# Hybrid decoder layer on one core: group A's second FFN takes its input without the norm's root, which multiplies gates and ups instead, and silu becomes one operation in the FFNs with quads

## The chip, the core and the metric

One core of a Trainium2 chip runs the whole layer in one launch, in fp32. The metric is the time of one execution on the device, in microseconds (us). TensorE (PE in the profile) multiplies matrices, VectorE (DVE), ScalarE (ACT) and GpSimd (POOL) work on elements, SyncE (SP) issues the transfers (DMA).

## The reference, cut to what matters

```python
D_MODEL = 1024; SEQ = 1024; N_META = 16; D_FF = 2816

def rms_norm(x, g):
    y = x * lax.rsqrt(jnp.mean(x * x, axis=-1, keepdims=True) + RMS_EPS)
    return y * g

def swiglu(h, w_gate, w_up, w_down):
    return (jax.nn.silu(h @ w_gate) * (h @ w_up)) @ w_down

h = concatenate([meta, x])                      # 1040 tokens
n = rms_norm(h, ffn1_norm)
h = h + 0.5 * swiglu(n, ffn1_w_gate, ffn1_w_up, ffn1_w_down)
proj = rms_norm(h, mix_norm) @ w_in
sb_out = stick_breaking_attention(q, k, v)      # 8 heads of 64, from proj
rw_out = rwkv7_time_mix(the other columns of proj)   # 8 heads of 64, a recurrence over the tokens
h = h + concatenate([sb_out, rw_out]) @ w_out
n = rms_norm(h, ffn2_norm)
h = h + 0.5 * swiglu(n, ffn2_w_gate, ffn2_w_up, ffn2_w_down)
return rms_norm(h, final_norm)[N_META:]
```

The root of rms_norm is one number per token, `lax.rsqrt(...)`; a product `n @ w` is that number times `(h * g) @ w`.

## The kernel before

**Products.** Each fp32 factor is split into two halves in TensorE's fast fp32 type: a high one (names that end in h or hi: nh, ah, whi) and the rest (nl, al, wlo). A product is three matrix instructions, high by high, low by high and high by low. Activations lie with the features on the 128 partitions and the tokens along the row; D_MODEL is 8 tiles (k), D_FF 22 tiles (f). Weights arrive as 512 KB tiles wraw of 128x1024; ScalarE copies the high half (whi), VectorE subtracts for the low one (wlo).

**Stages.** The tokens are two groups: A (16 meta and 512) and B (512). In order: FFN1 of A, projections of A, FFN1 of B with the mixer (attention and recurrence) of A laid between its products, projections of B, w_out of A (from about 1266 us to 1317 us), FFN2 of A with the mixer of B between its products and w_out of B late in it (1808 to 1853 us), FFN2 of B (from 1899 us), and the last norm. FFN1 of A and FFN2 of B are the two "fast" ones: most of their f tiles go in pairs, as quads (`gates2`, `ups2`), in which sums of weight and activation blocks stand for some of the products (qh, ql, t1, t2); sg is their sigmoid, cc the ring of tiles that it comes from.

**One FFN.** `gate` makes pg = n·w_gate in PSUM for a chunk of tokens (two chunks of 256 for the first f's, then 512 columns at once), takes sigmoid(pg) into sl on ScalarE, and multiplies sl by pg on VectorE. `up` makes pu, multiplies sl by it and splits the result into ah and al. `downs` makes pd from four f's at a time and adds half of it to h. 24 gates of this kind are in FFN2 of A: 4 on 256 columns, 20 on 512.

**The norm.** `norm_add` squares each new h tile (nsq) and adds up (nacc); `norm_sums` sums over partitions with TensorE (nps) and takes the inverse root on VectorE in a chain of small steps (fst); `norm_root` spreads it over the partitions (nyp on TensorE, ny by ScalarE). `norm_end` then makes, for each of the 8 k's, nf = h·gain·ny on VectorE, nh on ScalarE, and nl on VectorE or POOL in turn. In FFN2 of A this is done apart for two chunks of 256 tokens, as `norm_task("n2_0", i, ...)`, started by `hookC` when the chunk's last h tile has been added. `norm_raw`, which the norm ahead of the projections already uses, makes nh = h·gain and nl = h·gain − nh with no root.

**Order.** One instruction stream for each engine is written beforehand by a planner (`Clock`): tasks yield what they need, and the planner keeps a model of the engines' clocks and chooses what is issued next. All instructions are recorded through one helper, so nearly every row of the profile says L101 and is told apart by its tiles. Every engine works in the order given. Tiles with a tag share a ring of `bufs` buffers: nsq has 4, sl 2, ny 1, cc a few. Names in the mixer that the prediction uses: t, pz, pp, tt, lw, pe (decays and a small inverse), px, rsv, us (the recurrence over blocks), sgl and pgate (its output gate, read back from DRAM at lod), lt (read back from Ld).

Of the kernel before, what the change touches and what calls it, by code (L numbers as in the profile page):

```python
# [16 lines left out]
P = 128  # L17
# [434 lines left out]
class Ker:  # L452
# [279 lines left out]
    def norm_add(self, s, h, k, cols, now=True):  # L732

        nc, tp = self.nc, self.fp
        w = cols.stop - cols.start
        with self.urgent() if now else nullcontext():
            if s["k"] == 0:
                t = s["tile"]() if s["tile"] else tp.tile([P, 272], F32, tag="nacc", bufs=2, name="nacc")
                s["acc"] = t[:, :w]
                nc.scalar.activation(s["acc"], h[:, k, cols], AF.Square)  # L740
            else:
                sq = tp.tile([P, 272], F32, tag="nsq", bufs=4, name="nsq")[:, :w]
                nc.scalar.activation(sq, h[:, k, cols], AF.Square)
                if s["k"] >= KT - s["late"] and now and not s["tile"]:
                    s["last"].append(sq)
                    self.hold((sq,))
                else:
                    nc.vector.tensor_tensor(out=s["acc"], in0=s["acc"], in1=sq, op=ALU.add)
        s["k"] += 1
# [42 lines left out]
    def norm_end(self, s, h, cols, gain, n, bank, now=True):  # L792

        nc, tp = self.nc, self.fp
        w = cols.stop - cols.start
        ys = []

        def new():
            ys.append(tp.tile([P, 272], F32, tag="ny", bufs=1, name="ny"))
            self.hold(ys)  # L800
            return ys[0][:, :w]
        yield from self.norm_root(s, w, new, bank, ("ny", 1))
        y = ys[0][:, :w]
        for k in range(KT):
            yield from self.room(tp, ("sl", 2) if k % 2 else ("nsq", 4))
            with self.urgent() if now else nullcontext():
                f = tp.tile([P, 512], F32, tag="sl", bufs=2, name="nf")[:, :w] if k % 2 else tp.tile([P, 272], F32, tag="nsq", bufs=4, name="nf")[:, :w]
                nc.vector.scalar_tensor_tensor(f, h[:, k, cols], self.v(gain, k), y, ALU.mult, ALU.mult)
                self.split(n[0][k][:, cols], n[1][k][:, cols], f, nc.gpsimd if k % 2 else None)
        self.drop(ys)  # L810
        yield self.need(*[x for k in range(KT) for x in (n[0][k][:, cols], n[1][k][:, cols])])
# [41 lines left out]
            self.drop((xn,))  # L853


    def ffn(self, nm, h, n, chunks, edge, bank, first=None, hook=None, wx=False, poll=None, resid=None, done=None, wy=False, fast=False, once=False):

# [29 lines left out]
        def gate(w, c0, c1):  # L889
            pg = yield from mm(*w, "pg", c0, c1)  # L890
            with self.urgent():
                sl = tp.tile([P, 512], F32, tag="sl", bufs=2, name="sl")[:, :c1 - c0]
                nc.scalar.activation(sl, pg, AF.Sigmoid)
                nc.vector.tensor_tensor(out=sl, in0=pg, in1=sl, op=ALU.mult)
            self.hold((sl,))
            return sl

# [9 lines left out]
        def gates(f):  # L907
            if poll:
                yield from poll(f)
            w = yield from gu(gw, f)  # L910
            sls = []
            for c in chunks:
                sl = yield from gate(w, *c)
                sls.append(sl)
            return sls
        two = lambda w, f: (w[:, :, f * P:f * P + P], w[:, :, f * P + P:f * P + 2 * P])

        def gates2(f):

            yield lambda: self.fast and self.fast.k == 4  # L920
            c = self.fast
            x2 = yield from self.quad("pg", two(gw, f), bank)
            for x in x2:
                yield from self.room(c.p, ("cc", c.nc))
                with self.urgent():
                    sg = c.p.tile([P, 2 * c.w], F32, tag="cc", bufs=c.nc, name="sg")
                    nc.scalar.activation(sg, x, AF.Sigmoid)
                    nc.vector.tensor_tensor(out=x, in0=x, in1=sg, op=ALU.mult)
            self.hold(x2)
            return x2  # L930

# [52 lines left out]
        for part in PARTS:  # L984
# [49 lines left out]
            if f1 == NFT and hook:  # L1034
                yield from last(part)
            elif not (fast and f1 >= QF):
                for q in range(f1 - f0):
                    yield from downs(part, q)
        for op, x, f in quad_order() if fast else ():
            if op == "d":  # L1040
# [184 lines left out]
    def plan(self):  # L1225
# [13 lines left out]
        def ffn(nm, poll=False, wx=False, fast=False, once=False):  # L1239
# [7 lines left out]
            for f0, f1 in PARTS:  # L1247
# [16 lines left out]
                if f1 < NFT:  # L1264
# [1 line left out]
                        F["woutat"] = f1  # L1266
                        yield from wout(True)
                    yield gu("gate", f1)
                yield from [down(f0, f1, q) for q in range(f1 - f0)]
            for op, x, f in quad_order() if fast else ():  # L1270
                if op == "d":
                    yield down(*x, f)
# [785 lines left out]
    def body(self):  # L2058
# [64 lines left out]
        def xfirst():  # L2123

            with self.urgent():
                nc.sync.dma_start(out=g1r, in_=A["ffn1_norm"])
                xs.extend(xload(0, *b) for b in blks[:2])
                nc.scalar.activation(g1w, self.ones[:, 0:1], AF.Square)
            self.g1p = []
            for q in range(2):  # L2130
                yield self.need(g1r, bank=self.tbank)
                ps = tb("pg1")
                self.g1p.append(ps)
                self.hold((ps,))
                nc.tensor.matmul(ps, lhsT=self.ones[0:1, :], rhs=g1r[:, 512 * q:512 * q + 512], start=True, stop=True)
            F["g1b"] = True
            yield lambda: F.get("xn")
            for q, ps in enumerate(self.g1p):
                nc.scalar.activation(self.g1b[:, 512 * q:512 * q + 512], ps, AF.Copy)
            self.drop(self.g1p)  # L2140
# [130 lines left out]
        def wait(key):  # L2271
            def w(i):
                yield lambda: F.get((key, i))
            return w
# [62 lines left out]
        def poll(f=None):  # L2337

            if F.get("woutat", -1) == f and not F.get("wout"):
# [3 lines left out]

                def hook(i, m):
                    if hk(i, m):
                        norm_task("n2_1", i, f2["h"], chB, "g2", f2["n"], not late)
                yield from self.wout(f2["h"], f2["n"], hook, lambda i: F.get(("mixb", i)), late)

        def dense():
# [37 lines left out]
            F["stage"] = True  # L2387
            addC = add("n2_0", h, chB)

            def hookC(i, m):  # L2390
                if addC(i, m):
                    norm_task("n2_0", i, h, chB, "g2", n)
            yield from self.wout(h, n, hookC, lambda i: F.get(("mixl", i)))
            fsum = []

# [6 lines left out]
            def done(m):  # L2402
# [3 lines left out]
                if F["fsum"]:  # L2406
                    for i in range(2):
                        addF(i, m)
            yield from self.ffn("ffn2", h, n, ch, chB, bank, wait("n2_0"), None, None, poll, done=done)
            yield lambda: "woutat" in F  # L2410
            yield from poll()

            def fin0():
                yield lambda: F.get(("n2_1", 1))
                for i in range(2):
                    for m in () if F["fsum"] else range(KT):
                        yield from self.room(fp, ("nsq", 4))
                        addF(i, m)
                    yield from self.final(ssq["fin0", i], 0, h, slice(*chB[i]), bank, (fp, ("sl", 2)))
                    self.drop(fsum[i:i + 1])  # L2420
# [52 lines left out]
```

## Time and profile before

| | us |
|---|---|
| runs | 2272.85 (median), 2270.57, 2273.04 |
| profiled execution, its time | 2273.33 |
| its span in the trace | 2271.4 |
| TensorE busy | 2239.5 (99%) |
| VectorE busy | 1566.0 (69%) |
| ScalarE busy | 1085.4 (48%) |
| GpSimd busy | 555.8 (24%) |
| mean granted clock of TensorE | 0.994 |

A row of a timeline reads: start in us, duration in us, engine, line, operation, out<-in, shapes, and in brackets how long the engine was idle before it and what released it. A row of waits reads: engine and tile that waited, who released it, us in total, times, longest. A row of a group gives the count, the least, median and largest duration in ns, and the first and last start in us. In a stretch, the granted clock of TensorE is a share of full speed; a TensorE row counts its instruction's time from start to modelled end, and consecutive matrix instructions overlap, so what one costs is the distance between two starts.

### The profile page before, as it was taken

How to read it: one execution, taken by the hardware profiler on the slowest of the kernel's cores; microseconds unless marked ns; L12 is line 12 of the kernel's file. 1: busy time of each engine (PE TensorE's matmuls, PEld its weight loads, DVE VectorE, ACT ScalarE, POOL GpSimd, SP SyncE). 2: the span in 40 equal slices, each digit the busy share in tenths (PEclk: the TensorE clock that was granted, in tenths of full speed). 3: DMA queues.
4: the chain of work that ended last, by engine and by line, in shares of the span. 5: the costliest groups of instructions: out<-in, count | busy, mean ns of one | idle time of the engine just before them, and what ended most of it. 6: DMA issues, size and time to landing. Idle time of an engine off the chain costs nothing.

```text
span 2271.4 us, 41476 instructions
## 1 busy us (share of the span) xinstructions
PE 2239.5 (99%) x16303; PEld 1979.7 (87%) x16303; DVE 1566.0 (69%) x2673; ACT 1085.4 (48%) x2157; POOL 555.8 (24%) x700
## 2 busy tenths in 40 slices
PE   8999999999999999999999999999999999999998
PEld 7999999999878888778788987887877899899998
DVE  6888887475666655676476877547777656688885
ACT  6444444434343534555434554445666335354444
POOL 1322120013133231431012415324443001231110
PEclk9999999999999999999999989999999999999999
DMA  5543332545633233322545524333221433333332
GB/s 166 180 112 103 93 94 78 170 132 145 182 105 106 74 100 98 100 88 67 172 141 175 159 79 128 86 92 116 76 85 52 144 112 126 91 109 109 105 90 78
DMA packets 407384, 256.54 MB, mean 113 GB/s; under 512 B 44941, under 2 KB 392293, under 8 KB 407190
## 3 DMA queue, kind: packets, MB, share of 16 engines
q1 hardware_dynamic: 407190, 253.90, 38.2%
q8 instruction: 128, 2.10, 0.4%
q14 instruction: 66, 0.54, 0.1%
HBM read 219.85 MB, written 33.99 MB: 112 GB/s over the span
## 4 chain that ended last, share of the span: by engine, by line
PE 94%; DVE 2%; ACT 1%; DMA 1%; issue 1%; SPq 0%; POOL 0%; DVEq 0%; ACTq 0%; POOLq 0%
PE pd L101 34%; PE pu L101 22%; PE pg L101 21%; PE pwo L101 4%; PE px L101 3%; PE po L101 2%; PE pz L101 2%; PE pat L101 2%; PE pG L101 1%; DVE wlo L101 1%; PE psw L101 0%; DMA wraw<-in_ffn_w_gate_dram 0%; SPq L101 0%; PE pp L101 0%; ACT whi L101 0%
## 5 line engine op out<-in xcount | busy, mean ns | idle before, releaser
L101 ACT ACTIVATE whi<-wraw 128x1024 fp32r<-128x1024 f32 x314 | 330.6, 1053 | 333.9 <-PE pd L101 208.8
L101 DVE TENSOR_TENSOR wlo<-wraw,whi 128x1024 fp32r<-128x1024 f32 (+1 forms) x312 | 401.0, 1287 | 88.6 <-ACT whi L101 83.8
L101 PE MATMUL pd<-ah,whi 128*128 128x512 f32 (+2 forms) x944 | 325.9, 345 | 2.6 <-DVE h L101 1.2
L101 PE MATMUL pd<-ah,wlo 128*128 128x512 f32 (+2 forms) x944 | 319.3, 338 | 1.2 <-DVE wlo L101 1.2
L101 PE MATMUL pd<-al,whi 128*128 128x512 f32 (+2 forms) x944 | 318.5, 337 | 0.1
L101 PE MATMUL pd<-nh,whi 128*128 128x256 f32 (+7 forms) x648 | 210.6, 325 | 0.3 <-DVE st L101 0.2
L101 PE MATMUL pu<-nh,whi 128*128 128x512 f32 (+3 forms) x576 | 207.0, 359 | 0.0
L101 PE MATMUL pd<-nl,whi 128*128 128x256 f32 (+7 forms) x648 | 204.5, 316 | 0.0
L101 PE MATMUL pd<-nh,wlo 128*128 128x256 f32 (+7 forms) x648 | 204.4, 315 | 0.0
L101 PE MATMUL pg<-nh,whi 128*128 128x512 f32 (+3 forms) x536 | 199.8, 373 | 0.5 <-ACT nh L101 0.5
L101 PEld LDWEIGHTS pd<-ah,whi 128*128 128x128 f32 x944 | 177.6, 188 | 25.5 <-issue 3.1
L101 PE MATMUL pu<-nh,wlo 128*128 128x512 f32 (+3 forms) x576 | 198.6, 345 | 0.6 <-DVE wlo L101 0.6
L101 PE MATMUL pu<-nl,whi 128*128 128x512 f32 (+3 forms) x576 | 198.7, 345 | 0.0
L101 PEld LDWEIGHTS pd<-ah,wlo 128*128 128x128 f32 x944 | 177.6, 188 | 22.5 <-DVE wlo L101 2.1
L101 PEld LDWEIGHTS pd<-al,whi 128*128 128x128 f32 x944 | 177.8, 188 | 17.9 <-DVE al L101 0.7
L101 PE MATMUL pg<-nl,whi 128*128 128x512 f32 (+3 forms) x536 | 190.5, 355 | 0.9 <-DVE nl L101 0.9
L101 PE MATMUL pg<-nh,wlo 128*128 128x512 f32 (+3 forms) x536 | 190.2, 355 | 0.0
L101 POOL TENSOR_TENSOR qs<-wraw 128x512 f32<-128x512 f32 x60 | 101.5, 1697 | 359.3 <-DVE ql L101 142.3
L101 DVE SCALAR_TENSOR_TENSOR h<-pd,h 128x256 f32<-128x256 f32 (+1 forms) x200 | 107.4, 541 | 75.3 <-PE pd L101 73.9
L101 POOL TENSOR_TENSOR al<-sl,ah 128x512 fp32r<-128x512 f32 (+2 forms) x47 | 75.6, 1609 | 323.3 <-ACT ah L101 323.2
L101 PEld LDWEIGHTS pd<-nh,whi 128*128 128x128 f32 (+2 forms) x648 | 120.1, 185 | 13.0 <-issue 3.1
L101 PEld LDWEIGHTS pd<-nh,wlo 128*128 128x128 f32 (+2 forms) x648 | 120.1, 185 | 8.7
(393 smaller groups left out, 5624.6 us busy)
## 6 DMA issues: line engine op xcount, KB each, us to landing
wraw<-in_ffn_w_gate_dram SPq DMA_DIRECT2D x90, 512.0 KB
wraw<-in_ffn_w_up_dram SPq DMA_DIRECT2D x90, 512.0 KB
wraw<-in_ffn_w_down_dram SPq DMA_DIRECT2D x88, 512.0 KB
wraw<-in_w_in_dram SPq DMA_DIRECT2D x54, 512.0 KB
wraw<-in_w_out_dram SPq DMA_DIRECT2D x18, 512.0 KB
s<-rkvd SPq DMA_DIRECT2D x18, 256.0 KB
raw<-qkvd SPq DMA_DIRECT2D x16, 264.0 KB
raw<-qkvd SPq DMA_DIRECT2D x16, 256.0 KB
```

The lines of the kernel that those rows point to most:

```text
L101: self._c.trace(self._n, op, lambda: f(*a, **k), out, [x for x in args if isinstance(x, bass.AP)], k)
```

## The change

- `ffn` gets `root=`. Group A's second FFN is called with it; its input n is now h·gain in two halves, made by `norm_raw` from `hookC` for all 8 k's at once when the last w_out tile of a chunk has been added.
- A new task `norm2(i)` computes the root of a chunk into its half of `root2`, a tile of the ring ny, which is held until the last gate (f = 21) has been written.
- In `gate`, pg is multiplied by the root in PSUM before the sigmoid, and sl by the root once more after silu, which scales the up.
- In FFNs with quads, sigmoid and multiply become one Silu on ScalarE, in `gate` and, in place in PSUM, in `gates2`; sg is gone.
- nsq has 3 buffers instead of 4; the norm of group B's second FFN takes its pieces as urgent for chunk 0 only; group B's w_out may also be started between the downs of the last part.

```diff
     def norm_end(...):
-            ys.append(tp.tile([P, 272], F32, tag="ny", bufs=1, name="ny"))
+            ys.append(tp.tile([P, 512], F32, tag="ny", bufs=1, name="ny"))
...
-    def ffn(..., fast=False, once=False):
+    def ffn(..., fast=False, once=False, root=None):
...
         def gate(w, c0, c1):
             pg = yield from mm(*w, "pg", c0, c1)
             with self.urgent():
+                if root:
+                    nc.vector.tensor_tensor(out=pg, in0=pg, in1=root()[:, c0:c1], op=ALU.mult)
                 sl = tp.tile([P, 512], F32, tag="sl", bufs=2, name="sl")[:, :c1 - c0]
-                nc.scalar.activation(sl, pg, AF.Sigmoid)
-                nc.vector.tensor_tensor(out=sl, in0=pg, in1=sl, op=ALU.mult)
+                nc.scalar.activation(sl, pg, AF.Silu if fast else AF.Sigmoid)
+                if not fast:
+                    nc.vector.tensor_tensor(out=sl, in0=pg, in1=sl, op=ALU.mult)
+                if root:
+                    nc.vector.tensor_tensor(out=sl, in0=sl, in1=root()[:, c0:c1], op=ALU.mult)
             self.hold((sl,))
             return sl
...
+            if root and f == NFT - 1:
+                self.drop((root(),))
...
         def gates2(f):
             for x in x2:
-                yield from self.room(c.p, ("cc", c.nc))
                 with self.urgent():
-                    sg = c.p.tile([P, 2 * c.w], F32, tag="cc", bufs=c.nc, name="sg")
-                    nc.scalar.activation(sg, x, AF.Sigmoid)
-                    nc.vector.tensor_tensor(out=x, in0=x, in1=sg, op=ALU.mult)
+                    nc.scalar.activation(x, x, AF.Silu)
...
                 def hook(i, m):
                     if hk(i, m):
-                        norm_task("n2_1", i, f2["h"], chB, "g2", f2["n"], not late)
+                        norm_task("n2_1", i, f2["h"], chB, "g2", f2["n"], i == 0)
...
+            root2 = []
+
             def hookC(i, m):
                 if addC(i, m):
-                    norm_task("n2_0", i, h, chB, "g2", n)
+                    for k in range(KT):
+                        self.norm_raw(h, k, slice(*chB[i]), "g2", n)
+                    task(norm2(i), ("n2_0", i))
+
+            def norm2(i):
+                if i == 0:
+                    yield from self.room(fp, ("ny", 1))
+                    root2.append(fp.tile([P, 512], F32, tag="ny", bufs=1, name="root2"))
+                    self.hold(root2)
+                yield lambda: root2
+                yield from self.norm_root(ssq["n2_0", i], 256, lambda: root2[0][:, 256 * i:256 * i + 256], bank)
...
-            yield from self.ffn("ffn2", h, n, ch, chB, bank, wait("n2_0"), None, None, poll, done=done)
+            yield from self.ffn("ffn2", h, n, ch, chB, bank, wait("n2_0"), None, None, poll, done=done, root=lambda: root2[0])
```

**How the order moves.** TensorE's sequence from about 400 us to the end of group A's w_out, and its last rows, stay as they are. Three places show what moved; in the rows the numbers behind a name tell tiles apart (nh_147 and nh_148 hold the first and the second four k's), and "x2" is the count of like instructions.

TensorE at the end of group A's w_out, where the gate of f = 0 begins, before:

```order
L101 MATMUL pwo<-nh_148,wlo 128x256
L101 MATMUL nps<-ones,nacc 128x1 x2
L101 MATMUL pz<-t_15294,ab 32x32 x16
L101 MATMUL nps<-ones,nsq 128x1 x2
L101 MATMUL pg<-nh_147,whi 128x256
L101 MATMUL pg<-nl_149,whi 128x256
```

And now:

```order
L101 MATMUL pwo<-nh_148,wlo 128x256
L101 MATMUL nps<-ones,nacc 128x1 x2
L101 MATMUL pz<-t_15250,ab 32x32 x16
L101 MATMUL pg<-nh_147,whi 128x256
L101 MATMUL pg<-nl_149,whi 128x256
L101 MATMUL pg<-nh_147,wlo 128x256
```

The first gate's products no longer come behind the second chunk's last sum (nps from nsq), which now stands nine products later.

VectorE at the same place, before:

```order
L101 SCALAR_TENSOR_TENSOR nf<-h,vec,ny 128x256
L101 TENSOR_TENSOR h<-pwo,h 128x256
L101 TENSOR_TENSOR nl_150<-nf,nh_148 128x256
L101 TENSOR_TENSOR nacc<-nacc,nsq 128x256
L101 SCALAR_TENSOR_TENSOR nf<-h,vec,ny 128x256 x3
L101 SCALAR_TENSOR_TENSOR t_15294<-pp,half,t_15294 32x8x16 x2
L101 TENSOR_TENSOR nl_150<-nf,nh_148 128x256
L101 TENSOR_TENSOR h<-pwo,h 128x256
L101 TENSOR_TENSOR wlo<-wraw,whi 128x1024 x2
```

And now:

```order
L101 TENSOR_TENSOR bk<-a,pinv 64x8x64
L101 TENSOR_TENSOR h<-pwo,h 128x256
L101 SCALAR_TENSOR_TENSOR nl_149<-h,vec,nh_147 128x256 x4
L101 SCALAR_TENSOR_TENSOR nl_150<-h,vec,nh_148 128x256 x2
L101 TENSOR_SCALAR fst<-nps 128x2
L101 SCALAR_TENSOR_TENSOR nl_150<-h,vec,nh_148 128x256
L101 TENSOR_SCALAR fst<-fst 128x2
L101 SCALAR_TENSOR_TENSOR nl_150<-h,vec,nh_148 128x256
L101 SCALAR_TENSOR_TENSOR fst<-fst 128x2
L101 TENSOR_TENSOR wlo<-wraw,whi 128x1024
L101 TENSOR_TENSOR fst<-fst 128x2
L101 TENSOR_TENSOR pg<-pg,root_15288 128x256
```

Chunk 0's pieces, which stood between the h updates, are gone from here (they stand some 25 rows earlier); chunk 1's nl follow the last h at once, ahead of the up weights' low half, and the first multiply by the root follows.

TensorE in FFN2 of A where the root of group B's chunk 0 is spread (nyp), before, right behind w_out of B:

```order
L101 MATMUL pg<-nh_147,whi 128x512
L101 MATMUL pg<-nl_149,whi 128x512
L101 MATMUL pg<-nh_147,wlo 128x512
L101 MATMUL nyp<-ident,fst 128x128 x2
L101 MATMUL pg<-nh_148,whi 128x512
L101 MATMUL pg<-nl_150,whi 128x512
```

And now, in the last up:

```order
L101 MATMUL pu<-nh_148,whi 128x256
L101 MATMUL pu<-nl_150,whi 128x256
L101 MATMUL pu<-nh_148,wlo 128x256
L101 MATMUL nyp<-ident,fst 128x128 x2
L101 MATMUL pu<-nh_148,whi 128x256
L101 MATMUL pu<-nl_150,whi 128x256
```

The spread waits until the last gate has given up the ring ny; it moved behind the last gate, just ahead of the last downs.

More of the change, by code (lines that the diff above doesn't have):

```diff
@@ L741, in norm_add @@
             else:
-                sq = tp.tile([P, 272], F32, tag="nsq", bufs=4, name="nsq")[:, :w]
+                sq = tp.tile([P, 272], F32, tag="nsq", bufs=3, name="nsq")[:, :w]
                 nc.scalar.activation(sq, h[:, k, cols], AF.Square)
@@ L804, in norm_end @@
         for k in range(KT):
-            yield from self.room(tp, ("sl", 2) if k % 2 else ("nsq", 4))
+            yield from self.room(tp, ("sl", 2) if k % 2 else ("nsq", 3))
             with self.urgent() if now else nullcontext():
-                f = tp.tile([P, 512], F32, tag="sl", bufs=2, name="nf")[:, :w] if k % 2 else tp.tile([P, 272], F32, tag="nsq", bufs=4, name="nf")[:, :w]
+                f = tp.tile([P, 512], F32, tag="sl", bufs=2, name="nf")[:, :w] if k % 2 else tp.tile([P, 272], F32, tag="nsq", bufs=3, name="nf")[:, :w]
                 nc.vector.scalar_tensor_tensor(f, h[:, k, cols], self.v(gain, k), y, ALU.mult, ALU.mult)
@@ L853, in block, with ffn @@
             self.drop((xn,))
-    def ffn(self, nm, h, n, chunks, edge, bank, first=None, hook=None, wx=False, poll=None, resid=None, done=None, wy=False, fast=False, once=False):
+    def ffn(self, nm, h, n, chunks, edge, bank, first=None, hook=None, wx=False, poll=None, resid=None, done=None, wy=False, fast=False, once=False, root=None):
         nc, A, tp = self.nc, self.A, self.fp
@@ L1037, in ffn @@
                 for q in range(f1 - f0):
+                    if poll and q and f1 == NFT:
+                        yield from poll(f1 + q)
                     yield from downs(part, q)
@@ L1268, in ffn @@
                     yield gu("gate", f1)
-                yield from [down(f0, f1, q) for q in range(f1 - f0)]
+                for q in range(f1 - f0):
+                    if f1 == NFT and q and poll and F.get("f2b") and "woutat" not in F:
+                        F["woutat"] = f1 + q
+                        yield from wout(True)
+                    yield down(f0, f1, q)
             for op, x, f in quad_order() if fast else ():
@@ L2127, in xfirst @@
                 xs.extend(xload(0, *b) for b in blks[:2])
-                nc.scalar.activation(g1w, self.ones[:, 0:1], AF.Square)
+                nc.scalar.activation(g1w, self.ones[:, 0:1], AF.Silu)
             self.g1p = []
@@ L2416, in fin0 @@
                     for m in () if F["fsum"] else range(KT):
-                        yield from self.room(fp, ("nsq", 4))
+                        yield from self.room(fp, ("nsq", 3))
                         addF(i, m)
```

## Prediction, made before the changed kernel ran

> **What bounds the kernel now.** I read the totals and the chain that ended last, then TensorE's waits, then the stretches where its clock drops, and last VectorE, which gets most of the new work.
>
> ```profile
> PE 2239.5 (99%) x16303; PEld 1979.7 (87%) x16303; DVE 1566.0 (69%) x2673; ACT 1085.4 (48%) x2157; POOL 555.8 (24%) x700
> PE 94%; DVE 2%; ACT 1%; DMA 1%; issue 1%; SPq 0%; POOL 0%; DVEq 0%; ACTq 0%; POOLq 0%
> ...
> PE px L101 <- DVE rsv L101: 3.0, 5, 1.6
> PE pxn L101 <- DVE xn L101: 2.3, 2, 1.7
> ...
> PE nps L101 <- ACT nsq L101: 1.8, 2, 1.2
> PE pd L101 <- DVE wlo L101: 1.2, 2, 0.9
> ...
> PE pgate L101 <- DMA sgl<-lod: 1.1, 1, 1.1
> ...
> PE pg L101 <- DVE ql L101: 1.0, 1, 1.0
> PE pwo L101 <- DVE h L101: 1.0, 1, 1.0
> ...
> PE pz L101 <- DVE t L101: 0.8, 1, 0.8
> PE pu L101 <- DVE wlo L101: 0.6, 1, 0.6
> ```
>
> TensorE is the bound: the chain lies on it for 94%. It is idle for 2271.4 − 2239.5 = 31.9 us in the whole span, and no single kind of wait (us in total, times, longest) is above 3 us. The change leaves the count of matrix products as it is, so a gain can only come from some of these 31.9 us or from stretches at a low clock; a loss comes from new waits. The place where both meet is the end of group A's w_out:
>
> ```profile
> 1319.25 1.07 PE L101 MATMUL pz<-t,ab 32*32 32x32 f32 x32 [0.84 <-DVE t L101]
> 1321.51 1.01 PE L101 MATMUL nps<-ones,nsq 128*128 128x1 f32 x4 [1.20 <-ACT nsq L101]
> ...
> 1322.96 0.41 PE L101 MATMUL pg<-nh,wlo 128*128 128x256 f32 x1
> 1323.17 0.41 PE L101 MATMUL pg<-nh,whi 128*128 128x256 f32 x1
> ...
> 1342.08 0.28 PE L101 MATMUL pg<-nh,wlo 128*128 128x256 f32 x1
> 1342.19 0.28 PE L101 MATMUL pg<-nh,whi 128*128 128x256 f32 x1
> 1318.00:1322.00 4.00, 1.83 (x39) 1.52 (x38) 3.90 (x9) 3.13 (x8) 2.00 (x3) 0.86 0.00 0
> 1322.00:1334.00 12.00, 12.00 (x84) 11.71 (x84) 7.60 (x22) 4.78 (x13) 0.00 (x0) 0.50 0.31 89
> 1334.00:1336.00 2.00, 2.00 (x16) 2.00 (x16) 0.94 (x3) 0.87 (x3) 0.00 (x0) 0.86 0.06 15
> ...
> 1322.00:1334.00 12.00, 2.38 (x12) 2.61 (x12) 0.61 (x3) 0.27 (x1) 0.50 0.31 89
> 1336.00:1348.00 12.00, 3.52 (x24) 3.06 (x24) 1.76 (x7) 0.95 (x4) 1.00 0.14 43
> ```
>
> The rows after the products are stretches: length, busy time of PE, PEld, DVE, ACT, POOL, then the granted clock (the last two for the tile px alone, without POOL). TensorE is busy for 1.83 of 4 us, and the clock then stays at 0.50 for 12 us and returns in the next two. The same product starts every 0.21 us there and every 0.11 to 0.12 us at 1342.
>
> Who made it wait? VectorE, which was writing the normalized input just then:
>
> ```profile
> 1317.67 1.26 DVE L101 SCALAR_TENSOR_TENSOR nf<-h,vec,ny 128x256 f32<-128x256 f32 x3
> 1318.86 0.71 DVE L101 SCALAR_TENSOR_TENSOR t<-pp,half,t 32x128 f32<-32x128 f32 x2
> 1319.60 0.89 DVE L101 TENSOR_TENSOR nl<-nf,nh 128x256 fp32r<-128x256 f32 x1
> 1320.52 0.42 DVE L101 TENSOR_TENSOR h<-pwo,h 128x256 f32<-128x256 f32 x1
> 1320.86 2.35 DVE L101 TENSOR_TENSOR wlo<-wraw,whi 128x1024 fp32r<-128x1024 f32 x2
> ...
> 1318.18 1.21 ACT L101 ACTIVATE nh<-nf 128x256 fp32r<-128x256 f32 x3
> 1321.04 0.42 ACT L101 ACTIVATE nsq<-h 128x256 f32<-128x256 f32 x1 [0.71 <-DVE h L101]
> ```
>
> Chunk 0's nf and nl stand ahead of t (for pz), and ahead of the last h, whose square the last sum waits for.
>
> **The change, part by part.** The durations:
>
> ```profile
> L101 DVE SCALAR_TENSOR_TENSOR nf<-h,vec,ny x16: 472/477/956, 1311.4 to 1344.7; 128x256 f32<-128x256 f32 x16
> L101 DVE TENSOR_TENSOR nl<-nf,nh x8: 409/416/887, 1312.6 to 1343.5; 128x256 fp32r<-128x256 f32 x8
> L101 DVE TENSOR_TENSOR sl<-pg,sl x24: 405/691/694, 1332.2 to 1873.5; 128x512 f32<-128x512 f32 x20, 128x256 f32<-128x256 f32 x4
> L101 ACT ACTIVATE sl<-pg x24: 365/598/602, 1330.9 to 1872.5; 128x512 f32<-128x512 f32 x20, 128x256 f32<-128x256 f32 x4
>   ACT sl L101: 22.6, 12
> 1350.00:1800.00 450.00, 447.29 (x2893) 360.59 (x2892) 306.01 (x440) 234.21 (x458) 161.45 (x173) 1.00 0.33 95
> L101 DVE TENSOR_TENSOR cc<-cc,sg x32: 674/692/1803, 148.4 to 2219.4; 128x528 f32<-128x528 f32 x16, 128x512 f32<-128x512 f32 x16
> 2045.00:2050.00 5.00, 4.32 (x37) 4.12 (x35) 4.98 (x10) 3.15 (x7) 0.00 (x0) 1.00 0.01 2
> 1767.75 0.39 PE L101 MATMUL pd<-ah,whi 128*128 128x512 f32 x1
> 1767.98 0.40 PE L101 MATMUL pd<-al,whi 128*128 128x512 f32 x1
> 19.13 1.28 ACT L101 ACT_TABLE_LOAD   x1
> ```
>
> *The norm without its root.* 16 nf multiplies (0.477) become 16 nl of the same form, and the 8 VectorE subtractions (0.416, 3.3 us) and as many of POOL go. VectorE gains little; what counts is order. Chunk 0's pieces no longer wait for the root, and stand in one run of eight at about 1302.7 instead of 1311 to 1320; chunk 1's stand at about 1318.4, behind the last h, instead of at 1336 to 1345.
>
> - At 1302.7 eight nl (8 × 0.477 = 3.8 us) push back the scan, h and the weight halves behind them. TensorE waits there for h already (the pwo wait of 1.0), and the next product has the other bank. Between nothing and 1 us; I take +0.5.
> - At 1317.8, t now has no nf ahead of it, so the pz wait of 0.84 mostly goes. In the new order nine gate products (9 × 0.117 = 1.1 us) run before the last sum, which still waits: h 0.42, five nh of about 0.4, nsq 0.42 make 2.8 us, against pz's 1.07 and these 1.1, so about 0.9 is left of 1.20. The up weights' low half stands behind eight nl: 0.42 + 3.8 + 1.2 = 5.4 us after 1317.9, while TensorE has some 5 us of work; 0.3 more. Waits of 0.84 + 1.20 turn into 0.0 to 0.2 + 0.9 + 0.3; between −2 and +1, I take −0.8.
> - The low clock: its idle time is now split by full-size products, two of them at most 0.9. I take it that the clock stays up. What that is worth: 33 products of 256 columns between 1322.4 and 1335 save 33 × (0.213 − 0.118) = 3.1 us; all work at half of the speed for 12.6 us would save 6.3. The small products between them save less than half (px took 2.38 / 12 = 0.198 us each here and 3.52 / 24 = 0.147 at 1336). Between 3.1 and 6.3; I take −4.5.
> - Between 1336 and 1348 px, pu and their wlo wait for VectorE among nf and nl. These go; the multiplies by the root (0.405 on 256 columns) come instead, one at a time. The pu wait of 0.6 and part of px's go: 0 to −1.6, I take −0.9.
>
> The Trainium skill (TensorE: Matmul & The Clock Gate, Part 1: The HAM clock gate) says that the clock halves after an idle window of about 3.4 us and is whole again after about 3.4 us of sustained work. Here no idle piece is over 1.20 us and the half clock lasts about 13 us, so the trace disagrees with both lengths; by the page's length the gain would be 1.7 us instead of 4.5 and the sum 2.8 us higher.
>
> *The root on gates and ups.* Each of the 24 gates gets two more VectorE multiplies: 20 × 2 × 0.691 + 4 × 2 × 0.405 = 30.9 us, less the 3.3 above. VectorE goes from 306 to about 334 of 450 us, 68% to 74%, while TensorE is busy 447. The gate's chain gets longer by 0.69 ahead of the sigmoid (0.598), and 0.69 after the old multiply. Beside it run 24 up products of 512 columns, 24 × 0.23 = 5.5 us, before the next use of sl. VectorE now sits idle 22.6 us (12 times) waiting for that very sigmoid; part of the new work falls in there. What is late when VectorE falls behind is wlo: only two waits, 1.2 us together, are of that kind before. Bounds: 0, as nearly everything is covered, and 24 gates each adding the 0.69 of one multiply, 16.6 us. I take +1.0, near the waits that the trace shows.
>
> On SP's queue one more transfer (lt<-Ld) stands ahead of sgl's in the new order at about 1361; pgate waits 1.1 for sgl already. Bounds −1.1, if the products ahead of it last longer, and +2, if it lands late by a second such wait; I take +0.6.
>
> *Silu as one operation.* 32 multiplies of quads (0.692) go, 22 us, and 20 at the edge gates, about 9 more. Almost none of it was waited for. One wait answers: pg<-ql 1.0 at 2050, where VectorE is busy 4.98 of 5 us with quad halves and these multiplies; −1.0 (0 to −1.0). No row has a silu; its nearest is the sigmoid (0.598), and were it twice that, ScalarE, 48% busy, would be late by 0.6 for a value that an up needs some us later: 0. At the start the edge gates' multiplies stand among the first xn and nl (pxn waits 2.3 in all): −0.5 (0 to −1).
>
> Table loads go from two to three, 1.28 each, one moves to about 407 and one to about 1903. At 407 it stands ahead of a store of the low-rank columns, behind which TensorE has other weights' products; at 1903 ahead of the first silu, which only the ups need. I take 0; both uncovered would be +2.6.
>
> *The second group's norm* waits for the ring that the root holds, and moves from 1856 to the last downs. Its last piece now stands among the last h updates, about 10 us ahead of 1899, where its first reader begins. Cover: these last downs. 0; if it were late, by one nf, nh and nl, some 1.3 us. The ring of squares that goes from 4 to 3, and the extra chances for group B's w_out, leave the order there as it was: 0, or one more square's wait, 0.4.
>
> Sum: +0.5 − 0.8 − 4.5 − 0.9 + 0.6 + 1.0 − 1.0 − 0.5 = −5.6. The profiled execution took 2273.3 (span 2271.4), so 2267.7; its time is 0.5 above the median of the runs, 2272.85, which gives 2267.2. I say 2267.3.
>
> **The rivals.**
>
> *The clock drops all the same* (0.25). For it: 0.9 + 0.3 of waiting stay, and TensorE's small products leave it half empty; also the first long wait, pgate's, could grow. Against it: pgate's 1.1 and ql's 1.0 stand among full products, and the rows show no drop behind them. Without the −4.5 the sum is −1.1: 2271.8, no change.
>
> *VectorE becomes the bound of the second FFN* (0.12). At 74% with an order fixed beforehand, a gate's second multiply can hold up a wlo that TensorE is about to need. From 2266.3, the sum without its +1.0, it takes 11.1 us, or 0.46 in each of 24 gates, to be slower by 0.2%. At the full 0.69 per gate: 2266.3 + 16.6 = 2283. Against it: 22.6 us of VectorE's waiting for sigmoids, and TensorE waits for wlo only twice.
>
> *More goes than I count* (0.10): all 2 us at 1317 to 1322, the low clock at 6.3, px's and xn's waits: 0.5 − 2.0 − 6.3 − 1.6 − 1.0 − 1.0 = −11.4, 2261.5.
>
> *The forecast* has 0.53, with its own range of 2263 to 2270.5.
>
> **How the numbers follow.** A change under 0.2% (4.5 us) can hardly be told from none here: faster means below 2268.3. Of the forecast's 0.53 some 0.40 lies below that; with 0.10 of the larger gain and 0.03 of the clock's rival, faster has 0.53. The same: 0.13 + 0.21 + 0.02 = 0.36. Slower: 0.10 of VectorE's rival, 0.01 of the clock's, 0.11. The range from 2261.5 to 2275 takes the larger gain's time and the clock's rival with some waiting in the gates, and leaves out about 0.1 on the slow side and 0.06 below.
>
> **What would show it.** A clock of 1.00 from 1316 to 1340; waits of TensorE at pz below 0.3 and at the last nps about 0.9; nothing left of px's waits among nf; pg<-ql gone; VectorE at 330 to 336 of 450 us in the second FFN, with the waits for wlo there below 3 us in all; three table loads and no wait of TensorE beside them; the first gate of group B at its place behind the last downs. It is wrong if the clock falls to 0.50 behind 1318, or if waits for wlo, sl or al add up to more than 5 us between 1350 and 1900.

## The result: slower by about 0.4%, and the profile after

| | median, us | runs | against the kernel before |
|---|---|---|---|
| before, beside the first | 2274.80 | 7 | |
| changed kernel | 2280.76 | 7 | 1.0034 [1.0022, 1.0046] |
| before, beside the second | 2273.65 | 20 | |
| changed kernel, again | 2285.14 | 6 | 1.0047 [1.0033, 1.0062] |

The forecast was 2267.3, a gain of 0.25%; the range ended at 2275. The span of the profiled execution grew by 8.5 us, from 2271.4 to 2279.9. First the page's totals and its chain, then the longest waits of TensorE in the changed kernel (us in total, times, longest):

```profile
PE 2243.8 (98%) x16303; PEld 1983.9 (87%) x16303; DVE 1553.3 (68%) x2661; ACT 1088.8 (48%) x2158; POOL 541.7 (24%) x692
PE 37%; DVE 3%; ACT 1%; issue 1%; DMA 0%; SPq 0%; DVEq 0%; ACTq 0%
...
PE pp L101 <- issue: 3.1, 4, 1.3
PE pd L101 <- DVE h L101: 3.0, 5, 0.8
PE pg L101 <- DMA g1r<-in_ffn_norm_dram: 2.4, 1, 2.4
PE psw L101 <- ACT sw L101: 2.3, 1, 2.3
PE px L101 <- DVE rsv L101: 2.2, 4, 1.6
PE pxn L101 <- DVE xn L101: 2.0, 2, 1.8
PE pg L101 <- DVE h L101: 1.9, 1, 1.9
```

The chain is followed back over only 42% of the span here; TensorE still has nearly all of it. VectorE works 12.7 us less than before, and TensorE waits more: 2279.9 − 2243.8 = 36.1 us instead of 31.9. The waits at pz, nps (after nsq) and ql that the prediction named are gone from the top; psw, pp and the first gate (pg, for h) have come in.

**Where the time went.** The n-th product of a tile name such as pd or pwo is at fixed anchors the same piece of work in all traces, so the difference of its start in two traces tells what a stretch lost. In brackets stand TensorE's waits in that stretch and the time at half clock in it, both in us; the stretches are named by their times in the kernel before.

```
stretch, us       before        before_again   changed        changed again   own_ring_2     silu_only
0 to 1253         0             +1.2           +0.6           +5.5            +0.5           +0.9
1253 to 1317      0 (2.2, 0)    +2.4 (2.7,3.4) -0.5 (1.7, 0)  -0.2 (1.7, 0)   +2.1 (2.5,3.4) +2.1 (2.3,3.4)
1317 to 1811      0 (6.7,13.7)  -7.9 (4.6, 0)  +5.7 (9.7,17.1) +10.1 (13.2,20.5) +4.1 (9.5,13.7) -8.5 (4.3, 0)
1811 to 1853      0             0              0              0               +0.2           0
1853 to 1937      0 (0, 0)      0 (0, 0)       +4.0 (2.9, 0)  +4.0 (2.9, 0)   +0.1 (0, 0)    0 (0, 0)
1937 to 2077      0 (1.0, 0)    0 (1.0, 0)     -1.3 (0, 0)    -1.3 (0, 0)     -1.0 (0, 0)    -1.3 (0, 0)
span              2271.4        2267.1         2279.9         2289.6          2277.7         2264.7
```

Three things are to be read from it. A fixed loss of 4.0 us stands between 1853 and 1937, where the norm of group B's last FFN has moved. A fixed gain of 1.3 us stands near 2050, where silu took multiplies off VectorE. And between 1317 and 1811 stands a loss that differs from one execution to the next, as it does in the kernel before: two executions of one order lie 8 us apart there. Waits plus half of the time at half clock account for it: before 6.7 + 6.8 = 13.5, changed 9.7 + 8.6 = 18.3, changed again 13.2 + 10.3 = 23.5, before_again 4.6; the differences to the first, +4.7, +9.9 and −8.9, are near the +5.7, +10.1 and −7.9 measured.

Runs without a trace have a span and a mean granted clock on record too, and (1 − clock) times the span is an estimate of what half clock took. On average it is 14.2 us for the kernel before (73 runs on four chips, clock 0.9938) and 18.3 us for the changed kernel (13 runs, 0.9920); beside each other on one chip, 15.7 us (20 runs) and 19.8 us (6). So of the 10.4 us between the mean spans some 4 are half clock and some 6 are not.

### The profile page after: what moved, and what is told of

The parts are those of the page before. It is cut to its first block, busy times and chain, and to the rows that moved or that the text cites. A ratio compares the mean times of both kernels' runs of the same rounds, so it can differ in the third digit from the quotient of the medians.

```text
span 2279.9 us, 41472 instructions
## 1 busy us (share of the span) xinstructions
PE 2243.8 (98%) x16303; PEld 1983.9 (87%) x16303; DVE 1553.3 (68%) x2661; ACT 1088.8 (48%) x2158; POOL 541.7 (24%) x692
## 5 line engine op out<-in xcount | busy, mean ns | idle before, releaser
L101 DVE TENSOR_TENSOR wlo<-wraw,whi 128x1024 fp32r<-128x1024 f32 (+1 forms) x312 | 394.8, 1266 | 101.6 <-ACT whi L101 93.9
L101 POOL TENSOR_TENSOR qs<-wraw 128x512 f32<-128x512 f32 x60 | 94.5, 1579 | 366.1 <-DMA wraw<-in_ffn_w_gate_dram 128.5
L101 PEld LDWEIGHTS pd<-nh,whi 128*128 128x128 f32 (+2 forms) x648 | 120.2, 185 | 12.7 <-issue 3.3
```

The lines of the kernel that those rows point to most:

```text
L101: self._c.trace(self._n, op, lambda: f(*a, **k), out, [x for x in args if isinstance(x, bass.AP)], k)
```

## The experiments

**The clock: the same orders again.** before_again and after_again are the two kernels unchanged.

> The kernel before once more, for its profile. Theory A (the half clock at 1322 is a matter of where a window of the clock's watch falls): the waits at pz (0.8) and nps (1.2) are there again, the half clock behind them lasts another number of pieces of 3.4 us, or is not there, and the span moves by up to 6 us with it. Theory B (these waits always cause 13.7 us of it): the same stretch again.

> The changed kernel once more, on the same chip as the next. Theory A (the waits are fixed by the order of instructions, the stretches of half clock are not): the waits at psw (2.3 us), pg (1.9 us), al and whi are the same to 0.1 us, the stretches of half clock lie and last differently by one or more pieces of 3.4 us, and the span differs by 1 to 4 us. Theory B (both are fixed): the same stretches, span within 1 us of 2279.9.

Stretches of before, before_again, the changed kernel and after_again, each from 1320 to 1340; for before_again the one from 1300 ahead of it; for the changed kernel and after_again also those from 1360 and 1400:

```profile
1320.00:1340.00 20.00, 18.20 (x144) 17.46 (x137) 14.07 (x34) 10.40 (x29) 2.40 (x4) 0.66 0.28 79
```
```profile
1300.00:1320.00 20.00, 18.30 (x284) 17.75 (x283) 17.38 (x37) 10.99 (x26) 4.85 (x5) 0.91 0.42 107
1320.00:1340.00 20.00, 18.16 (x206) 16.88 (x204) 18.46 (x48) 14.11 (x37) 5.73 (x7) 1.00 0.28 80
```
```profile
1320.00:1340.00 20.00, 18.98 (x158) 17.59 (x159) 15.48 (x42) 12.15 (x32) 1.10 (x3) 0.83 0.20 58
1360.00:1380.00 20.00, 17.66 (x92) 15.45 (x91) 14.59 (x34) 7.14 (x13) 8.42 (x14) 0.83 0.43 134
1400.00:1440.00 40.00, 38.48 (x437) 32.04 (x436) 26.25 (x55) 20.59 (x56) 17.64 (x40) 0.96 0.24 65
```
```profile
1320.00:1340.00 20.00, 17.57 (x177) 16.33 (x178) 16.02 (x40) 13.78 (x35) 0.31 (x1) 0.91 0.31 91
1360.00:1380.00 20.00, 17.63 (x111) 16.40 (x110) 14.74 (x33) 10.18 (x21) 10.20 (x20) 0.83 0.47 142
1400.00:1440.00 40.00, 36.41 (x413) 30.07 (x412) 26.25 (x51) 15.99 (x44) 9.65 (x15) 0.91 0.26 66
```

The granted clock is the third number from the end. The kernel before, run again in the same order, has none of the half clock behind 1320 on which the largest term of the prediction rested: it fell once, to 0.91 in the stretch ahead, for 3.4 us. TensorE was later there, and of pz's and nps's waits 0.4 us was left. In the traces' clock record every stretch of half clock inside a span lasts 3.4, 6.8, 10.2 or 13.7 us. Some waits bring one each time (1.64 us at 582 in all traces, 10.2 us of it in both executions of before, 13.7 in after_again; 2.3 us at psw, 6.8 or 10.2). Length alone does not decide it: a wait of 1.88 us at pg (aside, below) and one of 2.31 us at pu (silu_port) brought none. Near 1304 the same wait of 1.0 us brought one in some executions and none in others, and where it did (before_again, silu_only, own_ring_2), none followed at 1320. The Trainium skill (TensorE: Matmul & The Clock Gate, Part 1: The HAM clock gate) says that the watch is a free-running window of about 3.4 us, so that one kernel meets it at different places; the trace agrees with the length and with the scatter, though 1.64 us of waiting within a window was enough here.

In these two traces both halves of theory A hold for the waits with names (psw 2.3 and 2.4, pg 1.88 twice, al and whi the same). The span differed by 9.7 us, more than the 1 to 4 expected; 5.0 of them lie ahead of 1253. In own_ring_2 and tiny_vt below, pg's wait was only 0.62 and 0.60: a half clock near 1304 had made TensorE come later, so where the half clock falls moves such waits too.

One kind of wait was not fixed even here: pp, 0.75 us near 1407 and 3.30 the second time. It is put down to "issue": no releaser is seen. The record of transfers shows what goes with it. The page of the changed kernel lists 128 instruction packets on queue 8 (packets, MB, share), which makes 16 KB each, and one for every 255 of TensorE's 32606 matrix instructions and weight loads:

```profile
q8 instruction: 128, 2.10, 0.4%
```

The sixteen traces together have 48 "issue" waits of TensorE of 0.3 us or more, and in all 48 one such packet ends 1.0 to 1.7 us before TensorE goes on. Near 1407 the packet started 1.7 us before TensorE stopped, in after_again 0.7 us after it had. This points to TensorE waiting for its next instructions among small products that use them up fast; no run moved such a packet, so the cause is not shown.

**Silu alone, root alone.** silu_only is the kernel before with the two silu edits and the first activation; root_only is the changed kernel without them.

```diff
 silu_only, against before
-                nc.scalar.activation(sl, pg, AF.Sigmoid)
-                nc.vector.tensor_tensor(out=sl, in0=pg, in1=sl, op=ALU.mult)
+                nc.scalar.activation(sl, pg, AF.Silu if fast else AF.Sigmoid)
+                if not fast:
+                    nc.vector.tensor_tensor(out=sl, in0=pg, in1=sl, op=ALU.mult)
...
-                    nc.scalar.activation(sg, x, AF.Sigmoid)
-                    nc.vector.tensor_tensor(out=x, in0=x, in1=sg, op=ALU.mult)
+                    nc.scalar.activation(x, x, AF.Silu)
```

> The kernel before with silu as one operation in the FFNs with quads and nothing else. The ledger of the two traces gives the start -1.2 us, the wait for ql near 2050 -1.3 us, and +2.3 us at the first gates of the last FFN, where a table load stands. Theory A (the moved norm of group B's last FFN, not silu, costs the 2.3): span 2.5 us below before. Theory B (the table load costs them): span within 0.5 us of before.

> The changed kernel with sigmoid and multiply put back in the FFNs with quads: the root on gates and ups, the three squares and the held ring stay. Theory A (the root causes the loss): 9 to 11 us above before, more than the whole change, since silu's gain is missing. Theory B (silu's table loads and queues cause half of it): 3 to 6 us above before.

silu_only took 2266.64 (12 runs) against 2271.78 (18): 0.9984 [0.9975, 0.9993]. It beats both kernels. root_only took 2285.45 (6 runs): 1.0051 [1.0038, 1.0064], more than the whole change. Theory A is the nearer one for both: silu_only gains 5 us in the medians and 3.6 by the ratio (1.6 to 5.7) where 2.5 was expected, root_only loses 14 in the medians and 11.6 by the ratio where 9 to 11 was. The sigmoid of the quads in the kernel before, and silu in the changed kernel:

```profile
L101 ACT ACTIVATE sg<-cc x32: 620/636/648, 146.3 to 2218.8; 128x528 f32<-128x528 f32 x16, 128x512 f32<-128x512 f32 x16
```
```profile
L101 ACT ACTIVATE cc<-cc x32: 616/633/651, 144.9 to 2227.1; 128x528 f32<-128x528 f32 x16, 128x512 f32<-128x512 f32 x16
```

The median is 0.633 us against 0.636, so the multiply is saved whole. From about 410 us to 1900 us the order of instructions in silu_only is the kernel before's, but for two rows of TensorE, so that its trace is a third execution of that order in the stretch from 1317 on: −8.5 us, no half clock. Of its gain 1.3 us is the wait for ql, which is gone; by the runs' clocks some 1 us is half clock (12.1 us lost instead of 13.1, a difference within the noise). The start differs by less than 1 us, and where the rest is stays open.

root_only's waits between 1857 and 1945:

```profile
PE pu L101 <- ACT whi L101: 1.0, 1, 1.0
PE pd L101 <- DVE al L101: 0.8, 1, 0.8
PE pu L101 <- DVE wlo L101: 0.8, 1, 0.8
PE pd L101 <- ACT ah L101: 0.3, 1, 0.3
```

They are those of the changed kernel, row for row, with no third table load; and silu_only, which has that load at 1897 us, loses nothing in this stretch. The load costs nothing there.

**A buffer of its own for the moved norm.** own_ring and own_ring_2 are one kernel: the spread root (ny) of group B's last norm no longer shares a ring with root2, so the norm stands behind w_out of B again. TensorE's order is the changed kernel's but for four rows.

```diff
-            ys.append(tp.tile([P, 512], F32, tag="ny", bufs=1, name="ny"))
+            ys.append(yp.tile([P, 272], F32, tag="ny2", bufs=2, name="ny") if yp else tp.tile([P, 512], F32, tag="ny", bufs=1, name="ny"))
```

> The changed kernel, with the spread root of group B's last norm in two buffers of its own in the pool opened after attention, so that it need not wait for the ring that root2 holds; TensorE's order is the changed kernel's but for four rows, the norm's pieces stand behind w_out of B again. Theory A (the moved norm is what loses 4.0 us between 1853 and 1937): al, ah, whi and wlo waits at 1885 and 1911 gone, 3 to 4.5 us below the changed kernel. Theory B (the longer chain in the last gates loses them): within 1 us of the changed kernel.

> The kernel with the spread root of group B's last norm in buffers of its own, beside the changed kernel on one chip. Theory A: 3 to 4.5 us below the changed kernel in the median, as the stretch from 1853 to 1937 says. Theory B (something later takes it back): within 1.5 us of it.

No wait of TensorE is left between 1853 and 1937, and the stretch costs +0.1 instead of +4.0, in both traces. The times: own_ring 2280.70 (12 runs), 1.0032 [1.0021, 1.0044]; own_ring_2 2280.55 (8 runs), 1.0029 [1.0017, 1.0041], beside 2285.14 of the changed kernel on the same chip. That is 4.6 us less there, close to the 3 to 4.5 expected, and nothing against the changed kernel's first median. The stretch is shown by the traces; the total alone would not settle it.

**The multiplies without their time.** In these four the planner still sees the changed kernel, so that the order of every engine is the changed kernel's (tiny_bk adds one clearing step on GpSimd), and only the instructions named here differ when they are issued. tiny_both does both multiplies on one column; aside gives the first its full width on another tile, so that the sigmoid doesn't wait for it; tiny_vt and tiny_bk shrink one GpSimd and three VectorE steps of the recurrence.

```diff
 tiny_both
+                    self.clock.ghost = dict(out=pg[:, 0:1], in0=pg[:, 0:1], in1=root()[:, c0:c0 + 1])
                     nc.vector.tensor_tensor(out=pg, in0=pg, in1=root()[:, c0:c1], op=ALU.mult)
 aside
+                    self.clock.ghost = dict(out=root()[:, c0:c1], in0=root()[:, c0:c1], in1=root()[:, c0:c1], op=ALU.max)
```

> The changed kernel in its own order of instructions, with both multiplies by the root done on one column only; the root is left out of the other columns. Theory A (their time and waits on VectorE cause the 5.7 us lost between 1318 and 1811): 4 to 6 us below the changed kernel. Theory B (the new order alone loses it): within 1 us of the changed kernel.

> The changed kernel in its own order, with the multiply ahead of the sigmoid replaced by one of the same width on the root's own tile, so that VectorE works as long and the sigmoid does not wait for it; the root is left out of the gate. Theory A (ScalarE's queue stands at the sigmoid until VectorE has come to the multiply, and TensorE waits behind it, 2.3 us at 1366): 3 to 5 us below the changed kernel, that wait gone. Theory B (VectorE's load is what counts): within 1 us of the changed kernel.

tiny_both took 2281.88 (5 runs), 1.0041 [1.0029, 1.0053]; aside 2281.19 (7 runs), 1.0039 [1.0024, 1.0054]. Neither is faster than the changed kernel: theory A of both falls. Between 1317 and 1811, tiny_both still loses 3.5 us (waits 8.5) and aside 3.5 (waits 10.5). Five executions of the changed order lose 4.1 to 10.1 there, and tiny_vt and tiny_bk, which keep both multiplies whole, lose 1.2 and 3.2. So, as far as single traces tell, no part of the loss comes from the multiplies' time; it is in the order planned around them. What the multiply ahead of the sigmoid does is seen at one place. VectorE, GpSimd, ScalarE and TensorE of the changed kernel near 1363:

```profile
1362.10 1.87 DVE L101 TENSOR_SCALAR st<-st 128x8 f32<-128x8 f32 x2
1363.88 0.42 DVE L101 TENSOR_TENSOR pg<-pg,root 128x256 f32<-128x256 f32 x1
...
1362.91 1.04 POOL L101 TENSOR_TENSOR vt<-vt,bon 128x512 f32<-128x512 f32 x1
...
1364.34 0.39 ACT L101 ACTIVATE sl<-pg 128x256 f32<-128x256 f32 x1 [1.57 <-DVE pg L101]
1364.62 1.05 ACT L101 ACTIVATE whi<-wraw 128x1024 fp32r<-128x1024 f32 x1
1365.57 0.47 ACT L101 ACTIVATE sw<-psw,vec 128x256 f32<-128x256 f32 x1
...
1366.09 0.48 PE L101 MATMUL psw<-tw 32*128 32x256 f32 x1 [2.34 <-ACT sw L101]
```

Read backwards: psw waits for the bank that sw empties; sw stands behind a weight copy and the sigmoid on ScalarE; the sigmoid waits 1.57 us for VectorE's multiply; that stands behind two steps on 8 columns that end at 1363.97, with GpSimd's vt (1363.95). In aside the sigmoid waits 0.38 and psw 1.15:

```profile
1367.30 0.38 ACT L101 ACTIVATE sl<-pg 128x256 f32<-128x256 f32 x1 [0.38 <-PE pg L101]
...
1369.04 0.48 PE L101 MATMUL psw<-tw 32*128 32x256 f32 x1 [1.15 <-ACT sw L101]
```

tiny_vt takes away GpSimd's part:

> The changed kernel in its own order, with GpSimd's vt multiply at 1363 done on one column; that part of the recurrence's output is left out. Theory A (VectorE's small st step at 1362.9 stands until GpSimd's vt is done, the multiply by the root, the sigmoid, the weight's half and psw stand behind it): the st pair falls from 1.87 to below 0.9 us and TensorE's wait at psw from 2.3 to 1.0 to 1.6. Theory B (psw waits for the multiply or for the order alone): the wait at psw stays above 2.0.

```profile
1359.69 0.87 DVE L101 TENSOR_SCALAR st<-st 128x8 f32<-128x8 f32 x2
...
1362.95 0.48 PE L101 MATMUL psw<-tw 32*128 32x256 f32 x1 [1.62 <-ACT sw L101]
```

As theory A said: 1.87 falls to 0.87, and 2.34 to 1.62, at the edge of the 1.0 to 1.6 expected. It is not the half clock near 1304, which this trace has and the first one has not: own_ring_2 has it too, and there the pair takes 1.87 and psw waits 2.36. The time of tiny_vt, 2282.63 (10 runs), 1.0037 [1.0026, 1.0048], doesn't show that 0.7.

**The h update at the first gate.** VectorE and TensorE of the changed kernel at 1318:

```profile
1318.16 0.68 DVE L101 TENSOR_TENSOR bk<-a,pinv 64x512 f32<-64x512 f32 x1
1318.77 0.68 DVE L101 TENSOR_TENSOR bk<-kp,pinv 64x512 f32<-64x512 f32 x1
1319.46 0.69 DVE L101 TENSOR_TENSOR bk<-a,pinv 64x512 f32<-64x512 f32 x1
1320.18 0.42 DVE L101 TENSOR_TENSOR h<-pwo,h 128x256 f32<-128x256 f32 x1
...
1320.75 0.55 PE L101 MATMUL pg<-nh,whi 128*128 128x256 f32 x1 [1.88 <-DVE h L101]
```

> The changed kernel in its own order, with the three bk multiplies that stand ahead of the last h update of w_out done on one column each, and bk cleared on GpSimd before; that part of the recurrence is left out. Theory A (they hold up the h update that frees the first gate's bank): the wait of 1.9 us at the first gate falls below 0.5, and the clock may stay up there, 1.5 to 4.5 us below the changed kernel. Theory B (the wait is the square's or the weights'): the wait stays above 1 us under another name.

```profile
1323.64 0.36 PE L101 MATMUL pg<-nh,whi 128*128 128x256 f32 x1 [0.48 <-DVE h L101]
```

The wait falls from 1.88 to 0.48, with no half clock near 1304 that could have done it: theory A for the wait. No half clock follows at 1320, but that shows nothing, as none follows in aside either, with the wait of 1.88 in place. The time, 2281.94 (5 runs), 1.0038 [1.0024, 1.0052], is no better; the trace has 0.9 instead of 0.3 us of wait at a later pd, and half clock at other places.

**Other plans.** no_mult plans and runs the changed kernel without the two multiplies; unit_mult is the kernel before with two multiplies by one in each gate; port_price and silu_port let the planner keep VectorE's tensor_scalar steps apart from GpSimd's work, on top of own_ring and of silu_only.

```diff
 port_price, silu_port
-        o.port = eng == "g" and op != "memset" or eng == "v" and op.startswith(("tensor_tensor", "scalar_tensor")) and \
+        o.port = eng == "g" and op != "memset" or eng == "v" and op.startswith(("tensor_tensor", "scalar_tensor", "tensor_scalar")) and \
```

> The changed kernel with neither multiply by the root, planned without them; the root is left out of the gates and ups. Theory A (the planner's answer to the two multiplies makes the waits between 1318 and 1811): 3 to 6 us below the changed kernel, waits at psw, pp and pd smaller. Theory B (the input that is ready earlier makes them, since the mixer and the gates are laid anew from 1302 on): within 1.5 us of the changed kernel.

> The kernel before with two multiplies by one, of the same sizes, in each gate of the second FFN of group A; norm, input and silu as before. Theory A (the multiplies and the order planned for them cause the loss): 3 to 7 us above before. Theory B (the early input causes it): within 2 us of before.

> The changed kernel with the spread root of group B's last norm in buffers of its own, and a planner that also keeps VectorE's tensor_scalar steps apart from GpSimd's work, as it does already with its two-tensor steps; everything is planned anew. Theory A (the waits in FFN2 of A come from a plan that does not know this wait): psw below 1 us, waits between 1318 and 1811 below 7 us in all instead of 9.7 to 13.2, 4 to 8 us below the changed kernel with own buffers. Theory B (24 gates with two more steps make a tight plan, whatever it knows): waits of 8 us and more stay, within 2 us of the kernel with own buffers.

> The kernel before with silu as one operation and the same addition to the planner. Theory A (a plan that knows this wait is better): 1 to 4 us below the kernel with silu alone. Theory B (the plan of the kernel before was already free of it at the places that matter, any new plan is a throw of the dice): anything from 3 us below to 6 above it.

| | median, us (runs) | against before | 1317 to 1811, us (waits, half clock) |
|---|---|---|---|
| no_mult | 2277.02 (11) | 1.0020 [1.0011, 1.0028] | −3.0 (8.2, 3.4) |
| unit_mult | 2306.41 (4) | 1.0145 [1.0128, 1.0162] | other pieces in the stretch |
| port_price | 2282.44 (7) | 1.0045 [1.0029, 1.0060] | +0.3 (8.3, 8.0) |
| silu_port | 2287.17 (6) | 1.0068 [1.0052, 1.0085] | other pieces in the stretch |

Without the multiplies the plan loses less: 4 to 8 us below the changed kernel's medians, 3 to 6 by the ratios, though its tail (1853 to 1937) costs 6.6 instead of 4.0. Its waits at psw and pp are smaller, as theory A said; those at pd are not (3.0 us instead of 2.2). Adding the multiplies to the kernel before, at its own late input, costs 34 us, and the trace shows where a part of them lies: w_out of B now comes at the end, and its weights are late (between 1800 and 1940, unit_mult):

```profile
PE pwo L101 <- DVE wlo L101: 6.0, 2, 5.2
PE pu L101 <- DVE wlo L101: 4.4, 1, 4.4
```

That is theory A of both in sign; in unit_mult it is five times the size. The planner's addition gives nothing: port_price keeps waits of 8.3 us (theory B), loses 5.1 us more from 1253 to 1317, and stands 0.13 to 0.16% (3 to 4 us) above the kernel with own buffers, where theory B allowed 2. silu_port, with no root at all, falls into the same late w_out as unit_mult (pwo waits 6.2 us, pu 2.3 there) and lands 0.84% above silu_only, far outside both theories. So unit_mult says little of the multiplies: a plan without any can end there. The planner's answer to a small edit can cost more than the edit.

## Why the prediction was wrong, step by step

I forecast 5.6 us less, and the medians are 6 and 11 us more. Three terms failed: the low clock that was to go (−4.5), the norm of group B that was to cost nothing (it cost 4.0), and the multiplies' +1.0, in whose stretch the waits alone rose by 4.8 and 7.9 us.

- *The pwo wait, +0.5.* It stayed at 0.95 instead of 1.0: nothing. *px, pu, wlo from 1336 on, −0.9*: these waits fell from 1.8 to 0.4 us in the first trace, −1.4: right.
- *The end of w_out, −0.8.* pz's wait went, as said. But I let h follow the last product at once ("h 0.42, five nh ..."), while three bk (2.0 us) stood ahead of it in the order, the last of them in the rows shown, and did not see that the first gate's bank is the one that this h frees. In place of 0.84 and 1.20 stands one wait of 1.88. And the two waits were no property of the order before: before_again has 0.4 us of them, silu_only 0.5.
- *The low clock, −4.5.* The largest term failed. I took 13.7 us of half clock in one execution for a property of the order. The kernel before loses it in one execution and not in another, 8 us apart in that stretch. No term of this size may rest on one trace; the changed kernel had 17.1 and 20.5 us of it, and over all runs half clock took some 4 us more from it than from the kernel before, where I had 4.5 less.
- *The two multiplies, +1.0.* The rival that I gave 0.12 was the nearer one, by another mechanism than I wrote. VectorE is busy 317.6 of 450 us there, not 334. The waits from 1350 to 1811 rose from 2.7 to 7.4 us in the first trace and to 10.6 in the second, with psw 2.3, pp 2.1 and pd behind h 1.8 in the first, and pp 4.6 in the second. The first trace of the changed kernel:

```profile
1350.00:1800.00 450.00, 442.49 (x2826) 357.70 (x2826) 317.56 (x463) 229.43 (x446) 160.62 (x170) 0.99 0.31 92
```

  I priced the chain of the gate and VectorE's load. I did not price what stands behind the sigmoid on ScalarE while it waits for VectorE (whi, sw, and TensorE's psw), nor that the planner lays everything behind 1350 anew, with pp's waits among the small products. Waits for wlo, which I named, did not come. (I wrote that the kernel before has two of them; my own rows show three, 1.8 us.)
- *sgl, +0.6.* pgate has no wait at all in the changed kernel (−1.1): my lower bound. That is luck rather than the change: before_again waits 0.4 there and silu_only nothing.
- *Silu, −1.0 at ql*: −1.3, right in kind and 0.3 beyond my bound. *The start, −0.5*: −0.6 and +0.6 in the two traces, so nothing that can be told. *Table loads, 0*: right, three loads, none beside a wait of TensorE.
- *Group B's norm, 0.* Wrong by 4.0, the clearest part. I checked that its last piece is ready 10 us ahead of its reader, but not what the moved pieces push back on VectorE and ScalarE: al and ah for the last downs (0.8 and 0.3) and the weights of the next FFN's first up (1.0 and 0.8), 2.9 us in all; the remaining 1.1 us has no row of its own. With a buffer of its own it is 0.1. Where a half clock of 3.4 us falls behind these waits (tiny_both, aside, tiny_bk), the stretch costs 5.5 to 5.6.

Sum of what the traces show: +4.0 for the norm, −1.3 for silu, and between 1317 and 1811 more waits and half clock. There the order of the kernel before was traced three times (before, before_again, silu_only: 0, −7.9, −8.5 us; half clock 13.7, 0, 0) and that of the changed kernel five times (with own_ring, own_ring_2 and root_only: +5.7, +10.1, +8.1, +4.1, +6.3; half clock 13.7 to 20.5), and four times more with a few steps shrunk or moved (+1.2 to +3.5; half clock 10.2 to 17.1). They don't overlap, but so few throws don't give a mean; the medians, 6 and 11 us above before, leave 3 to 9 for this stretch. That the order causes this, and not the multiplies' time, is what tiny_both shows; no_mult shows that a plan without them can lose less. Whether the planner's answer to the multiplies makes the loss, or any new plan would have, is not shown, since silu_port moved by 19 us with no multiply at all. Which row of the plan matters most is open too: every single wait that was shortened (psw, pg) left the total where it was.

## What to carry to other kernels

Look at more than one execution before a stretch of low clock is put into a sum: it may be a throw of the dice and still be the largest number on the page. Where a new step stands between two engines in order, price the queue behind the waiting instruction on the second engine; and where a longer hold moves work, price what that work displaces where it lands, not only whether its own reader is served. If a planner sets the order, take the part of an edit that leaves the order nearly alone (here silu, faster by 0.16%) and test the rest against a run with the order held fixed.

## What the hardware showed that I had not expected

- VectorE's small steps on st, 128x8, take 0.15 to 0.18 us where no GpSimd step runs beside them (55 in the changed kernel) and up to 1.2 us where one does (17). The five longest each end within 0.03 us of a GpSimd step (1363.97 and 1363.95 above; with that step on one column the pair fell by 1.0 us).
- Half clock comes in pieces of 3.4 us and can follow 1.64 us of waiting, or stay away behind 2.31; executions of one order differed by 8 us in the same 500 us through it and the waits that it shifts.
- A wait of TensorE that is put down to "issue" can go with a 16 KB instruction packet: in 48 of 48 such waits one ended 1.0 to 1.7 us before TensorE went on.
- Silu takes as long as a sigmoid (0.633 against 0.636 us on 512 to 528 columns), so that one operation stands for two at the price of one.
